# A subtraction emitted one product later in the MLP units of a hybrid decoder trunk

## The chip, the cores and the metric

The kernel runs on one core of a Trainium2 chip. The metric is the device time of one execution in microseconds (us). The engines are named as the profile names them: PE is TensorE (matmuls), PEld its weight loads, DVE is VectorE, ACT is ScalarE, POOL is GpSimd, and SP is SyncE, whose queue issues the DMAs.

## The reference

The reference is a decoder trunk of two layers over 528 tokens (16 meta tokens and 512 of the sequence) of width 1024. Layer 0 mixes with retention and gated DeltaNet heads, layer 1 with a Mamba-2 mixer. Behind each mixer stands a layer norm and an MLP with a squared ReLU, which is all that matters here:

```python
def sq_relu_mlp(h, w1, w2):
    return jnp.square(jax.nn.relu(h @ w1)) @ w2
...
h = layer_norm(DN_ALPHA * h + sq_relu_mlp(h, mlp_w1[i], mlp_w2[i]), ln2_w[i], ln2_b[i])
```

`w1` is 1024 x 4096 and `w2` 4096 x 1024.

## The kernel before, in words

**Split numbers.** All large products run on numbers that are split into a high part, rounded to the matmul's format, and a low part, the rest. A product of two such numbers takes three matmuls: high by high, high by low, low by high. Weights are split as they arrive: ScalarE rounds (line 152) and VectorE subtracts (line 153, function `split`). Activations are split where they are made.

**The MLP.** Features of the hidden layer are made in eight groups of four blocks of 128. Group 0 and half of group 1 are made by plain products (`phase`, lines 609 to 618). All other halves of groups, 13 per MLP and so 26 in the kernel, are made by a `Unit`: two blocks of 128 features by two halves of the tokens (264 columns each in layer 0, 256 in layer 1), by a fast scheme of seven products instead of eight. Each of the seven is 12 matmuls (line 514: four blocks of the contraction by three). They write to three PSUM banks in turn: `ba` (products 1, 3, 5, 7), `bc_` (2, 6) and `bb` (4). ScalarE copies `ba`, `bc_`, `ba` after products 1 to 3 (lines 518, 521, 524) into `x1`, `x2`, `x3`. VectorE adds product 4, 5 and 6 to these (lines 527, 531, 535). In order: product 4 onto `bb`, sum of line 527, output; product 5 onto `ba`, sum of line 531, output; product 6 onto `bc_`, sum of line 535, output; product 7 onto `ba`, output. `ba` keeps accumulating, so the seventh product adds to what the sum of line 531 reads.

**The output (`evac_u`).** For each of the four outputs ScalarE takes the ReLU (line 451), GpSimd squares it in full precision (line 453, into a tile `q`), ScalarE squares it into the high part (line 459), and VectorE subtracts the high part from `q` to give the low part (line 460). That last subtraction is what the change moves. `q` is a tile of the tag "m", which has 24 buffers; the high and low parts are of tag "s" with 40.

**The second product.** A stage `Four` multiplies four blocks of `w2` with a finished group and adds the result to the residual on VectorE (line 383; for a first contribution, line 385). Stages alternate: a `Unit` of group c, a `Four` of group c-1, and so on. In layer 0 a `Four` has matmuls of 272 and 256 columns, in layer 1 of 512.

**What sets the order.** The code emits instructions in an order written out by hand. After each product, and after each half of a block in a `Four`, it calls `adv`, which takes the next stage's preparation (weight fetches, additions of lines 487 to 491, splits) one step on and gives waiting tasks a turn (`tick`). A planner then orders each engine's instructions when the program is compiled: it runs through the program by durations of its own and gives an engine the earliest emitted of the instructions that are ready in its run, so the order on an engine can differ from the order of emission. On the chip each engine keeps the planner's order.

Of the kernel before, what the change touches and what calls it, by code (L numbers as in the profile page):

```python
# [12 lines left out]
F32 = mybir.dt.float32  # L13
# [3 lines left out]
ADD, SUB, MUL, MIN, MAX, POW = ALU.add, ALU.subtract, ALU.mult, ALU.min, ALU.max, ALU.pow  # L17
# [40 lines left out]
def trunk(ctx: ExitStack, tc: tile.TileContext, a, out):  # L58
    nc = tc.nc
    V, G, S, T, SY = nc.vector, nc.gpsimd, nc.scalar, nc.tensor, nc.sync  # L60
# [11 lines left out]
    def tl(tag, cols, dt=F32, part=P):  # L72
        return sb.tile([part, cols], dt, tag=tag, bufs=NBUF[tag], name=nm(tag))
# [4 lines left out]
    def pm(cols, part=P):  # L78
        return ps.tile([part, cols], F32, tag="mm", bufs=3, name=nm("pmm"))
# [30 lines left out]
    def tick():  # L110
        for gen in list(tasks):
            if gen in tasks:
                advance(gen)
# [117 lines left out]
    def parts(pair, spans):  # L231

        return [tuple(x[:, o:o + n] for x in pair) for o, n in spans]
# [189 lines left out]
    def mlp(l, hx, h, ns, ready, evac0, pairs, final=None):  # L423
# [4 lines left out]
        nh = (ns[0] + ns[1]) // 2  # L428
# [12 lines left out]
        def group():  # L441
            u = [[None] * GF for _ in hx]
            us = [None] * GF

            def evac_u(f, hf, o, n=None):
                if n is None:
                    n, off = ns[hf], hf * ns[0]
                else:
                    off = hf * n
                t = tl("m", n)  # L450
                S.activation(t, o, AF.Relu)  # L451
                q = tl("m", n)
                G.tensor_tensor(q, t, t, op=MUL)  # L453
                if us[f] is None:
                    us[f] = pair = tl("s", L, F32R), tl("s", L, F32R)
                    for dst, x in zip(u, parts(pair, ((0, ns[0]), (ns[0], ns[1]), (0, 512)))):
                        dst[f] = x
                hi, lo = [x[:, off:off + n] for x in us[f]]
                S.activation(hi, t, AF.Square)
                V.tensor_tensor(lo, q, hi.bitcast(F32), op=SUB)  # L460
            return u, evac_u

        def second_src(c, m):
# [2 lines left out]
        class Unit:  # L466
# [7 lines left out]
            def prepare(self):  # L474
# [26 lines left out]
                self.ops["s4"] = sp(s4)  # L501

            def run(self, adv):
                ba, bb, bc_ = pm(nh), px(nh), px(nh)
                row = tl("row", 1024)
# [11 lines left out]
                prod(ba, "a11", 0, True, False)  # L517
                S.copy(x1, ba)
                adv()
                prod(bc_, "s1", 4, True, False)  # L520
                S.copy(x2, bc_)
                adv()
                prod(ba, "s2", 5, False, False)
                S.copy(x3, ba)
# [62 lines left out]

        groups = [group() for _ in range(NG)]

        def unit(c, i):  # L590
            return Unit(c, i, lambda f, hf, o: groups[c][1](f, hf, o, nh))

        def four(c, i):
            return Four(c, groups[c][0], 4 * i)

        stages = [unit(1, 1), four(0, 0), four(0, 1)]
        for c in range(2, NG):
            stages += [unit(c, 0), four(c - 1, 0), unit(c, 1), four(c - 1, 1)]
# [23 lines left out]
        for i, st in enumerate(stages):  # L622
            if i + 2 < len(gens):
                next(gens[i + 2])

            def adv():
                next(gens[i + 1], None)
                tick()
            st.run(adv)
            for _ in gens[i + 1]:  # L630
                pass
        for _ in gens[-1]:
            pass
        if final is not None:
            final(groups[-1][0][2], last[0].blks, h)
            return
# [537 lines left out]
    r, ev = accumulate(r0)  # L1174
    hn, hx, ready1 = norm_after(r, ns0, PP_LN + 16, PP_LN + 24)
    mlp(0, h, r0, ns0, ready, ev, hp)
    h = hn

# [200 lines left out]
    for g in range(4):  # L1379
        f = []  # L1380
# [20 lines left out]
    for m in range(3):  # L1401
        blks = wload(srcs[m][0]) + wload(srcs[m][1][:, 0:512], 512)
        o = pm(512)
# [13 lines left out]
    def final(u, blks, r):  # L1417
# [41 lines left out]
        with tc.manual_schedule(engines=ORDERED):  # L1459
# [12 lines left out]
            store(3, 512, 704, t1[:, 0:192])  # L1472

    mlp(1, h, r0, ns1, ready, ev, hp, final)
    drain()

# [100 lines left out]
```

## Time and profile before

| | us |
|---|---|
| runs | 1718.58 (median), 1712.72, 1718.89 |
| profiled execution | 1710.59 |
| its span | 1708.8 |
| granted TensorE clock, mean | 0.994 |
| TensorE busy | 1662.7 (97%) |
| VectorE busy | 1154.1 (68%) |
| ScalarE busy | 739.0 (43%) |
| GpSimd busy | 316.9 (19%) |

The first MLP runs from about 530 to 890 us of the span, its units from 575 us on; the second from about 1360 us, its units from 1380 to 1665 us. A pair of `Unit` and `Four` repeats every 22.7 us in layer 0 (L553's fetches start at 656.49 and 679.19) and every 21.8 us in layer 1.

How to read the rows. A timeline row has the start in us from the span's start, the duration in us, the engine, the line of the kernel, the operation, the tiles written and read, the shapes and the number of instructions merged into the row; in brackets the idle time of that engine before it and what ended it. A row of the waits reads: engine, line, who was waited for, total us, number of times, the longest. A matmul's row lasts longer than the distance to the next one, since matmuls are pipelined.

### The profile page before, as it was taken

To read this page: it belongs to the slowest core of one execution; us is meant where nothing else is said; L and a number is where in the kernel's file an instruction comes from. 1 tells how busy PE (TensorE), PEld (TensorE's weight loads), DVE (VectorE), ACT (ScalarE), POOL (GpSimd) and SP (SyncE) were. 2 spreads that over 40 slices of the span, in tenths; PEclk is the share of its full clock that TensorE was granted. 3 is DMA by queue.
4 is the path that set the end of the run, shared out by engine and by line. 5 is a ranking of instruction groups with operands and counts; after the bars stand their busy time and mean duration, and the time that the engine had idled before them with its cause. 6 is when DMAs were issued, how large, how long until landed. Compare 5 with 4: busy or idle time off the path is not lost.

```text
span 1708.8 us, 29912 instructions
## 1 busy us (share of the span) xinstructions
PE 1662.7 (97%) x11884; PEld 1529.0 (89%) x11884; DVE 1154.1 (68%) x2300; ACT 739.0 (43%) x1509; POOL 316.9 (19%) x360
## 2 busy tenths in 40 slices
PE   9899999999999999999999999999999999999998
PEld 7898998899999999999998988888778888888886
DVE  5896667666437857766657776858553876666665
ACT  4432245554214534444434665656432544444441
POOL 1211210010003301111102034242410321111112
PEclk9999999999999999999999999999999999999999
DMA  6233212112222322222221443333222222222231
GB/s 219 83 95 93 70 38 69 50 51 79 95 75 69 106 93 96 81 97 99 88 71 63 139 117 110 108 111 112 68 86 96 79 99 93 98 94 96 92 116 49
DMA packets 88484, 155.60 MB, mean 91 GB/s; under 512 B 11864, under 2 KB 43224, under 8 KB 88344
## 3 DMA queue, kind: packets, MB, share of 16 engines
q1 hardware_dynamic: 88200, 153.53, 28.1%
q8 instruction: 93, 1.52, 0.4%
q14 instruction: 47, 0.39, 0.1%
q10 hardware_dynamic: 144, 0.16, 0.0%
HBM read 148.92 MB, written 4.75 MB: 90 GB/s over the span
## 4 chain that ended last, share of the span: by engine, by line
PE 81%; DVE 8%; ACT 3%; POOL 3%; issue 2%; DMA 2%; SPq 0%; POOLq 0%; DVEq 0%; ACTq 0%
PE pmm L178 19%; PE pmm L177 19%; PE pmm L176 19%; PE pmm L514 7%; PE pmx L514 4%; POOL m L453 2%; ACT w L152 1%; DVE w L153 1%; PE pmx L1439 1%; DVE s L650 1%; DMA w<-in_w 1%; PE pmx L1289 1%; ACT m L451 1%; DVE s L460 1%; PE pmx L1293 1%
## 5 line engine op out<-in xcount | busy, mean ns | idle before, releaser
L176 PE MATMUL pmm<-hh,w 128*128 128x256 f32 (+5 forms) x1480 | 455.2, 308 | 5.6 <-ACT s L643 2.0
L178 PE MATMUL pmm<-hh,w 128*128 128x256 f32 (+3 forms) x1480 | 443.4, 300 | 0.2 <-DVE w L153 0.2
L177 PE MATMUL pmm<-hl,w 128*128 128x256 f32 (+3 forms) x1480 | 442.0, 299 | 1.2 <-DVE hl L344 0.9
L153 DVE TENSOR_TENSOR w<-w,w 128x1024 fp32r<-128x1024 f32 (+2 forms) x253 | 312.3, 1236 | 147.7 <-PE pmm L177 79.8
L152 ACT CAST w<-w 128x1024 fp32r<-128x1024 f32 (+2 forms) x253 | 260.9, 1032 | 347.5 <-PE pmm L177 88.9
L176 PE MATMUL pmm<-s,w 128*128 128x256 f32 (+2 forms) x1136 | 361.2, 318 | 0.0
L178 PE MATMUL pmm<-s,w 128*128 128x256 f32 (+2 forms) x1136 | 360.8, 318 | 0.0
L177 PE MATMUL pmm<-s,w 128*128 128x256 f32 (+2 forms) x1136 | 360.3, 317 | 0.0
L176 PEld LDWEIGHTS pmm<-hh,w 128*128 128x128 f32 (+2 forms) x1480 | 279.0, 189 | 19.5 <-issue 4.2
L177 PEld LDWEIGHTS pmm<-hl,w 128*128 128x128 f32 (+1 forms) x1480 | 278.8, 188 | 12.5 <-issue 2.1
L178 PEld LDWEIGHTS pmm<-hh,w 128*128 128x128 f32 (+1 forms) x1480 | 279.0, 189 | 8.8 <-DVE w L153 0.7
L177 PEld LDWEIGHTS pmm<-s,w 128*128 128x128 f32 x1136 | 213.7, 188 | 14.3 <-DVE s L1368 0.3
L176 PEld LDWEIGHTS pmm<-s,w 128*128 128x128 f32 x1136 | 213.9, 188 | 14.0
L178 PEld LDWEIGHTS pmm<-s,w 128*128 128x128 f32 x1136 | 213.7, 188 | 14.1
L453 POOL TENSOR_TENSOR m<-m 128x256 f32<-128x256 f32 (+2 forms) x128 | 117.1, 917 | 534.3 <-ACT m L451 530.8
L147 POOL TENSOR_TENSOR n<-n,neg 128x1 f32<-128x1 f32 (+2 forms) x58 | 40.3, 699 | 439.3 <-DVE n L146 418.7
L650 DVE SCALAR_TENSOR_TENSOR s<-s,pp,s 128x528 f32<-128x528 f32 x120 | 102.2, 851 | 27.1 <-ACT s L648 24.9
L383 DVE TENSOR_TENSOR m<-m,pmm 128x272 f32<-128x272 f32 (+1 forms) x208 | 81.7, 415 | 19.1 <-PE pmm L178 19.0
L460 DVE TENSOR_TENSOR s<-m,s 128x256 fp32r<-128x256 f32 (+2 forms) x128 | 64.9, 508 | 43.9 <-POOL m L453 41.5
L514 PE MATMUL pmm<-s,s 128*128 128x264 f32 (+1 forms) x624 | 83.8, 283 | 0.1
L514 PEld LDWEIGHTS pmm<-s,s 128*128 128x128 f32 x624 | 78.5, 188 | 0.5 <-DVE s L153 0.3
L527 DVE TENSOR_TENSOR row<-row,pmx 128x264 f32<-128x264 f32 (+1 forms) x26 | 11.0, 424 | 97.2 <-PE pmx L514 97.2
(313 smaller groups left out, 2464.8 us busy)
## 6 DMA issues: line engine op xcount, KB each, us to landing
w<-in_w SPq DMA_DIRECT2D x88, 512.0 KB, 3.2
w<-in_mw SPq DMA_DIRECT2D x146, 256.0 KB, 3.1
w<-in_mw SPq DMA_DIRECT2D x38, 512.0 KB, 3.3
w<-in_wo SPq DMA_DIRECT2D x29, 512.0 KB, 3.3
row<-rd SPq DMA_DIRECT2D x16, 512.0 KB, 5.6
sp<-in_mw SPq DMA_DIRECT2D x26, 256.0 KB, 2.7
s<-rd SPq DMA_DIRECT2D x32, 128.0 KB, 5.8
w<-in_w2n SPq DMA_DIRECT2D x4, 512.0 KB, 3.2
```

The source lines that it names most:

```text
L147: G.tensor_tensor(dst, t, neg5[0:part, 0:n], op=POW)
L152: S.copy(dst_hi, src)
L153: V.tensor_tensor(dst_lo, src, dst_hi.bitcast(F32), op=SUB)
L176: T.matmul(o, w[0], x[0], start=first, stop=False)
L177: T.matmul(o, w[0], x[1], start=False, stop=False)
L178: T.matmul(o, w[1], x[0], start=False, stop=last)
L383: V.tensor_tensor(t, t, o, op=ADD)
L451: S.activation(t, o, AF.Relu)
L453: G.tensor_tensor(q, t, t, op=MUL)
L460: V.tensor_tensor(lo, q, hi.bitcast(F32), op=SUB)
L514: T.matmul(o, w[x][:, c], B[b][k][y], start=first and k == i == 0, stop=last and k == 3 and i == 2, skip_group_check=True)
L650: V.scalar_tensor_tensor(acc, cin[:, k:k + L], w[k], acc, op0=MUL, op1=ADD)
```

## The change

The low parts of the units' four outputs are no longer subtracted inside `evac_u`. The operands are put on a list, and `adv` emits what was put there one product earlier. So the low part of an output is emitted after the sum and the output of the following product. That of product 7 is emitted in the first `adv` of the next stage. The two plain phases, which do not pass a list, stay as they are.

```diff
-            def evac_u(f, hf, o, n=None):
+            def evac_u(f, hf, o, n=None, late=None):
...
                 S.activation(hi, t, AF.Square)
-                V.tensor_tensor(lo, q, hi.bitcast(F32), op=SUB)
+                if late is None:
+                    V.tensor_tensor(lo, q, hi.bitcast(F32), op=SUB)
+                else:
+                    late[-1].append((lo, q, hi.bitcast(F32)))
...
+        late = [[], []]
+
+        def lower():
+            for lo, q, hi in late.pop(0):
+                V.tensor_tensor(lo, q, hi, op=SUB)
+            late.append([])
+
         def unit(c, i):
-            return Unit(c, i, lambda f, hf, o: groups[c][1](f, hf, o, nh))
+            return Unit(c, i, lambda f, hf, o: groups[c][1](f, hf, o, nh, late))
...
             def adv():
+                lower()
                 next(gens[i + 1], None)
                 tick()
             st.run(adv)
...
         for _ in gens[-1]:
             pass
+        lower()
+        lower()
         if final is not None:
```

## The prediction

> **What bounds the kernel now.** I read the page's busy shares first, then TensorE's waits, then the chain of waits and the engines' timelines in one repeat of the multilayer perceptron (MLP).
>
> ```profile
> PE 1662.7 (97%) x11884; PEld 1529.0 (89%) x11884; DVE 1154.1 (68%) x2300; ACT 739.0 (43%) x1509; POOL 316.9 (19%) x360
> ...
> PE pmm L514 <- DVE row L531: 14.5, 26, 2.1
> PE pmx L1053 <- DVE m L1098: 2.8, 1, 2.8
> ...
> PE pmm L514 <- DVE row L531: 6.3, 12, 0.6
> ...
> PE pmm L514 <- DVE row L531: 5.6, 12, 0.5
> ...
> DVE s L460 <- POOL m L453: 41.5, 62, 0.9
> ```
>
> TensorE is busy 97% of the span, so time can only come from its gaps. The largest wait of TensorE by far is on line 531, VectorE's sum behind a unit's fifth product: 26 times, once in each of the 26 units; the next is a fifth of it. Two answers for stretches of the two MLPs, 605 to 890 and 1375 to 1660 us, show that 12 of the waits in each are alike (0.53 and 0.47 us in the mean); the first unit of layer 0 and the last of layer 1 stand outside of them. These rows count a wait from the end of a matmul's record, which lasts some 0.28 us while the next matmul can start 0.12 us after it, so that the time lost is larger than 14.5 us; it is worked out below from starts. Line 460, the subtraction that the change moves, waits for GpSimd's square on line 453. How the two are connected is seen in the repeat from 656 to 679 us:
>
> ```profile
> 662.13 1.64 PE L514 MATMUL pmm<-s,s 128*128 128x264 f32 x12
> ...
> 664.95 0.28 PE L514 MATMUL pmx<-hh,s 128*128 128x264 f32 x1
> 665.06 0.29 PE L176 MATMUL pmm<-s,w 128*128 128x272 f32 x1
> 665.87 0.51 PE L514 MATMUL pmm<-s,w 128*128 128x264 f32 x2 [0.51 <-DVE row L531]
> ...
> 664.95 0.19 PEld L176 LDWEIGHTS pmm<-s,w 128*128 128x128 f32 x1
> 665.86 0.30 PEld L514 LDWEIGHTS pmm<-s,w 128*128 128x128 f32 x2 [0.73 <-DVE row L531]
> ...
> 662.40 0.43 DVE L527 TENSOR_TENSOR row<-row,pmx 128x264 f32<-128x264 f32 x1 [4.41 <-PE pmx L514]
> 663.29 1.23 DVE L153 TENSOR_TENSOR w<-w,w 128x1024 fp32r<-128x1024 f32 x1 [0.46 <-ACT w L152]
> 665.04 0.43 DVE L460 TENSOR_TENSOR s<-m,s 128x264 fp32r<-128x264 f32 x1 [0.52 <-POOL m L453]
> 665.39 0.42 DVE L531 TENSOR_TENSOR row<-row,pmm 128x264 f32<-128x264 f32 x1
> 665.73 0.42 DVE L535 TENSOR_TENSOR row<-row,pmx 128x264 f32<-128x264 f32 x1
> 667.07 0.43 DVE L460 TENSOR_TENSOR s<-m,s 128x264 fp32r<-128x264 f32 x1 [0.92 <-POOL m L453]
> ...
> 663.66 1.34 POOL L453 TENSOR_TENSOR m<-m 128x264 f32<-128x264 f32 x1 [17.30 <-ACT m L451]
> 668.43 0.63 POOL L453 TENSOR_TENSOR m<-m 128x264 f32<-128x264 f32 x1 [0.45 <-ACT m L451]
> ```
>
> The fifth product of the unit ends at 662.13+1.64 = 663.77; from then on line 531 has its input. VectorE is in the weight split of line 153 until 663.29+1.23 = 664.52. Then comes line 460 for the fourth product, which waits until GpSimd's square is ready (663.66+1.34 = 665.00), and line 531 stands behind it: it starts at 665.39, 0.87 us after the split ended. The seventh product adds onto the bank that line 531 reads, so its weight load starts only at 665.86. TensorE has put in one matmul of the next stage (line 176, at 665.06) and then starts nothing until 665.87.
>
> **The change part by part.** It removes and adds no instruction. In each unit the four line 460 subtractions are emitted one product later: 26x4 = 104 moves, the same operands, the same 0.43 us. Line 460 of product 4 goes behind line 531, that of product 5 behind line 535, that of product 6 behind product 7, and that of product 7 behind the first product and sum (line 383) of the following stage. The last is also emitted behind the weight fetches with which that stage begins on SyncE's queue; SyncE waits for nothing of it, and no DMA is moved. On GpSimd nothing is passed that waits for line 460.
>
> Step 1, does VectorE's order follow? A planner orders VectorE: it takes a ready instruction ahead of one that it thinks not ready, as the rows show, where line 535 runs ahead of product 5's line 460, which the code emits earlier. Line 460 of product 4 must therefore have been ready in the plan when it was taken, and the code's order decided only if line 531 was ready too. On the chip line 531 has been ready for 664.52-663.77 = 0.75 us when the split ends. The plan has just one line 176 matmul between the sixth and seventh product, so its line 531 ends about when the sixth ends, 1.45 us (12 matmuls) after the fifth ended; line 460 starts in it some 0.35+0.42 us earlier, about 0.7 us after line 531's input. Both were ready, so the later emission swaps them.
>
> Step 2, what line 531 then costs. It starts as the split ends, at 664.44 (consecutive VectorE rows overlap by 0.08), and ends at 664.86. That GpSimd's square is running there must be allowed for. The nearest row is line 1326, of the same engine with one PSUM operand and 256 columns, of which the first instance below lies inside one GpSimd instruction and the third has none beside it:
>
> ```profile
> 1025.18 0.41 DVE L1326 SCALAR_TENSOR_TENSOR s<-m,pmm 128x256 f32<-128x256 f32 x1
> ...
> 1041.79 0.41 DVE L1326 SCALAR_TENSOR_TENSOR s<-m,pmm 128x256 f32<-128x256 f32 x1
> ...
> 1024.13 2.03 POOL L1302 TENSOR_TENSOR s<-s,s 128x512 f32<-128x512 f32 x1
> ```
>
> Both take 0.41 us, so I take 0.42 for line 531. The other end is that it waits for the square to finish: it then ends at 665.00+0.42 = 665.42. No reason makes it shorter than 0.41. [...]
>
> Step 3, does TensorE still wait? A weight load followed the end of line 531 by 0.05 us (665.81 to 665.86). From 664.86 that gives 664.91, and the free weight load after the sixth product is at 664.95: no wait in layer 0. So each of the 12 regular units there gives 665.87-665.06 = 0.81 less the usual 0.12 between matmuls, 0.69 us. In layer 1 the stage's matmuls have 512 columns:
>
> ```profile
> 1443.88 0.40 PE L176 MATMUL pmm<-s,w 128*128 128x512 f32 x1
> 1444.74 0.62 PE L514 MATMUL pmm<-s,w 128*128 128x256 f32 x3 [0.46 <-DVE row L531]
> ...
> 1442.20 1.23 DVE L153 TENSOR_TENSOR w<-w,w 128x1024 fp32r<-128x1024 f32 x1 [0.47 <-ACT w L152]
> ...
> 1446.44 0.23 PE pmm L177
> ...
> 583.83 0.28 PE L177 MATMUL pmm<-s,w 128*128 128x272 f32 x1
> 586.21 0.63 PE L514 MATMUL pmm<-s,w 128*128 128x264 f32 x3 [2.09 <-DVE row L531]
> ...
> 583.65 1.22 DVE L153 TENSOR_TENSOR w<-w,w 128x1024 fp32r<-128x1024 f32 x1
> ...
> 585.73 0.42 DVE L531 TENSOR_TENSOR row<-row,pmm 128x264 f32<-128x264 f32 x1
> ...
> 1662.43 0.40 PE L178 MATMUL pmm<-s,w 128*128 128x512 f32 x1
> 1663.27 0.75 PE L514 MATMUL pmm<-s,w 128*128 128x256 f32 x4 [0.43 <-DVE row L531]
> ```
>
> Its 12 regular units give 1444.74-1443.88 = 0.86 less the usual 0.23 of such a matmul, 0.63 us each. Line 531 would end at 1442.20+1.23-0.08+0.42 = 1443.77 and allow a weight load at 1443.82; a free one stands 0.11 ahead of 1443.88, at 1443.77, so at worst 0.05 us is left per unit. The first unit of layer 0 waits longer, since its split also comes late: line 531 moves from 585.73 to 583.65+1.22-0.08 = 584.79, 0.94 us, and the rest of its gap stays. The last unit of layer 1 gives 1663.27-1662.43 = 0.84 less 0.23, 0.61 us.
>
> Sum: 12x0.69 + 12x0.63 + 0.94 + 0.61 = 8.3+7.6+0.9+0.6 = 17.4 us, less up to 13x0.05 = 0.65 for layer 1: 17.0 us.
>
> Step 4, what the moved instruction costs where it lands. Product 4's line 460 still starts at about 665.02, when the square is ready, now behind line 531; line 535 follows at 665.37 instead of 665.73, and ScalarE's activations behind lines 531 and 535 come 0.95 and 0.36 us earlier. The lower parts are first read by a stage that runs after a further unit, over 10 us later. I cost this at nothing; what hides it is that distance and the idle 0.52 and 0.92 us ahead of line 460, and if that cover were gone, each moved instruction would cost VectorE its 0.43 us. Buffers: an output holds two of 24 "m" tiles, of which 16 are the residual; the 8 left serve four outputs, all that a unit has. Late next is TensorE itself, with matmuls at their usual distance through the unit.
>
> The profiled execution took 1710.59 us for its span of 1708.8, so it would take 1693.6. It is the lowest of the four times shown: the three runs have 1712.72, 1718.58 (the median) and 1718.89. From the median the sum gives 1701.6, from the mean of the four (1715.2) 1698.2. I forecast 1700.
>
> **The rivals.** (a) The order stays as it was, because in the plan line 460 is taken before line 531 has its input, by shorter times for the square than the chip's. For it: the chip's square takes twice as long beside the split as at 668.43, and a plan may not know that. Against it: the 0.7 us of step 1. Then the time is as before, 1712 to 1719. (b) Line 531 has to wait for the square after all (the other end of step 2): the weight load comes at 665.47 instead of 665.86, a gain of 0.39 us in 25 units and at most 0.94 in the first, 10.7 at most and some 9 us with a later plan: 1708 to 1709. Against it speaks line 1326. (c) Slower: with the new emission the plan fills VectorE's idle places with the preparation of the next unit, and the sums of the following stage (line 383) come later. The rows:
>
> ```profile
> 668.71 0.29 PE L178 MATMUL pmm<-s,w 128*128 128x272 f32 x1
> ...
> 667.42 1.12 DVE L491 TENSOR_TENSOR s<-w,sp 128x512 f32<-128x512 f32 x1
> ...
> 669.27 0.68 DVE L153 TENSOR_TENSOR s<-sp,s 128x512 fp32r<-128x512 f32 x1
> 669.87 0.42 DVE L383 TENSOR_TENSOR m<-m,pmm 128x272 f32<-128x272 f32 x1
> ```
>
> The first product of that stage ends about 669.0, its sum starts at 669.87, 0.9 us later; with three banks TensorE can run two products (2x1.45 = 2.9 us) ahead of a sum. Were line 491 and three splits of 512 columns (1.12+3x0.68 = 3.2 us) all put ahead of the first sum, it would be 4.1 us late and TensorE would wait 1.2 us per unit, 26x1.2 = 31 us, against the 17 gained: 1718.6+14 = 1733. It decides from 2.0 us of delay on, and makes the kernel slower than before from 2.0+17/26 = 2.7 us on. Against it: line 491 and one of the splits are ahead of that sum already, and VectorE's work in the stage begins 0.95 us earlier.
>
> **How the numbers follow.** My forecast 0.73, (a) 0.13, (b) 0.07, (c) 0.07. A difference of 0.5% is 8.6 us, about what a measurement of this kernel can tell from no change. Faster by more than that: the forecast and half of (b), 0.77; within it: (a) and the other half, 0.16; slower: (c), 0.07. The range takes in the forecast from its low end (1710.6-17.4 = 1693, with a margin of 1) and (b) up to 1709 with a margin of 2: 1692 to 1711, which leaves out (a) and (c).
>
> **What would show it.** On VectorE's timeline line 531 follows the split of line 153 directly and line 460 comes behind it, still waiting for GpSimd; TensorE's wait on line 531 falls from 14.5 us to under 2.5, almost all of it in the first unit; a repeat of unit and stage shortens from 22.7 us to 22.0 in layer 0; line 453 leaves the chain in favour of TensorE; line 383 is no later behind its product than before. The prediction is wrong if line 460 is still ahead of line 531, if line 531 takes more than 0.45 us, or if a new wait of TensorE on lines 176 to 178 or 514 has over 5 us.

## The result, and the profile after

| | before | after |
|---|---|---|
| runs, median (us) | 1715.65 (1709.34 to 1718.89, 4 runs) | 1691.51 (1689.14 to 1691.81, 4 runs) |
| profiled execution (us) | 1710.59 | 1691.81 |
| its span (us) | 1708.8 | 1690.0 |

The ratio after to before is 0.9861, with a 95% interval of 0.9827 to 0.9895: 24 us by these medians, 18.8 us by the two profiled spans. Both are more than the 17.0 us of the prediction's sum, and the time lies 0.5 us below the range. In the changed file the lines stand three (in the unit) lower: L517 is the old L514, L530, L534 and L538 are the sums of products 4, 5 and 6 (old L527, L531, L535), and L597 is the moved subtraction (old L460).

The page after: busy time of each engine, and the chain of work that ended last (before it had PE 81% and POOL 3%).

```profile
PE 1655.9 (98%) x11884; PEld 1528.5 (90%) x11884; DVE 1159.4 (69%) x2300; ACT 740.2 (44%) x1509; POOL 313.9 (19%) x360
...
PE 87%; DVE 7%; ACT 2%; DMA 2%; issue 1%; POOL 1%; SPq 0%; POOLq 0%; DVEq 0%; ACTq 0%
```

TensorE's waits after, the five largest:

```profile
PE pmm L176 <- ACT w L152: 3.5, 1, 3.5
PE pmx L1302 <- DVE s L1263: 2.8, 3, 1.3
PE pmx L801 <- DVE n L793: 2.6, 1, 2.6
PE pmx L1066 <- DVE m L1111: 2.6, 1, 2.6
PE pmm L517 <- DVE row L534: 2.0, 1, 2.0
```

The wait on product 5's sum is there once instead of 26 times, in the first unit, and in the MLPs no wait of its size has come in its place. The repeat that the prediction read, whose fifth product starts 0.9 us earlier in the span now (661.23 against 662.13), on the timelines of TensorE, VectorE and GpSimd:

```profile
661.23 1.64 PE L517 MATMUL pmm<-s,s 128*128 128x264 f32 x12
...
664.04 0.28 PE L517 MATMUL pmx<-hh,s 128*128 128x264 f32 x1
664.16 1.63 PE L517 MATMUL pmm<-s,w 128*128 128x264 f32 x12
665.63 0.29 PE L176 MATMUL pmm<-s,w 128*128 128x272 f32 x1
...
662.39 1.23 DVE L153 TENSOR_TENSOR w<-w,w 128x1024 fp32r<-128x1024 f32 x1 [0.46 <-ACT w L152]
663.53 0.42 DVE L534 TENSOR_TENSOR row<-row,pmm 128x264 f32<-128x264 f32 x1
664.36 0.43 DVE L538 TENSOR_TENSOR row<-row,pmx 128x264 f32<-128x264 f32 x1 [0.41 <-PE pmx L517]
664.71 1.04 DVE L597 TENSOR_TENSOR s<-m,s 128x264 fp32r<-128x264 f32 x2
...
668.09 0.42 DVE L383 TENSOR_TENSOR m<-m,pmm 128x272 f32<-128x272 f32 x1
...
662.87 1.23 POOL L453 TENSOR_TENSOR m<-m 128x264 f32<-128x264 f32 x1 [17.52 <-ACT m L451]
```

Line 534 starts 0.09 us before the split's row ends (662.39+1.23 = 663.62) and takes 0.42 us inside GpSimd's square (662.87 to 664.10). It is done at 663.95, before the sixth product's last matmul starts at 664.04, and the seventh product follows 0.12 us after that. Line 538 runs ahead of the moved subtractions, which stand in one row with those of product 5.

Beside it the same product before, and the pair in layer 1 (before, then after):

```profile
665.06 0.29 PE L176 MATMUL pmm<-s,w 128*128 128x272 f32 x1
665.87 1.75 PE L514 MATMUL pmm<-s,w 128*128 128x264 f32 x12 [0.51 <-DVE row L531]
...
1444.74 1.69 PE L514 MATMUL pmm<-s,w 128*128 128x256 f32 x12 [0.46 <-DVE row L531]
```

```profile
1432.59 0.28 PE L517 MATMUL pmx<-hh,s 128*128 128x256 f32 x1
1432.71 1.64 PE L517 MATMUL pmm<-s,w 128*128 128x256 f32 x12
...
1432.20 0.41 DVE L534 TENSOR_TENSOR row<-row,pmm 128x256 f32<-128x256 f32 x1
...
1432.66 0.42 PEld L517 LDWEIGHTS pmm<-s,w 128*128 128x128 f32 x3
```

The twelve matmuls of product 7 last 1.75 us behind a wait and 1.63 us without one in layer 0, 1.69 and 1.64 in layer 1. That is a loss that the prediction did not see. In layer 1 a small wait is left: the weight load of product 7 starts at 1432.66, 0.05 us after the sum's end (1432.20+0.41 = 1432.61), and the second matmul of product 7 comes 0.17 us after the first, where 0.12 is usual. Over all regular units, by TensorE's starts:

| mean, us | layer 0 before | after | layer 1 before | after |
|---|---|---|---|---|
| last start of product 6 to first of product 7 | 0.934 | 0.119 | 0.980 | 0.117 |
| first to third start of product 7 | 0.350 | 0.244 | 0.343 | 0.282 |
| one repeat of `Unit` and `Four` | 22.715 | 21.931 | 21.807 | 21.107 |

Before, the first row of this table holds one matmul of the next stage (0.12 us in layer 0, 0.23 in layer 1), which stands elsewhere after; so it is not all loss, and the last row is the gain.

### The profile page after: what moved, and what is told of

The parts are those of the page before. It is cut to its first block, busy times and chain, and to the rows that moved or that the text cites. A ratio compares the mean times of both kernels' runs of the same rounds, so it can differ in the third digit from the quotient of the medians.

```text
span 1690.0 us, 29900 instructions
## 1 busy us (share of the span) xinstructions
PE 1655.9 (98%) x11884; PEld 1528.5 (90%) x11884; DVE 1159.4 (69%) x2300; ACT 740.2 (44%) x1509; POOL 313.9 (19%) x360
## 4 chain that ended last, share of the span: by engine, by line
PE 87%; DVE 7%; ACT 2%; DMA 2%; issue 1%; POOL 1%; SPq 0%; POOLq 0%; DVEq 0%; ACTq 0%
PE pmm L176 20%; PE pmm L178 20%; PE pmm L177 20%; PE pmm L517 9%; PE pmx L517 6%; PE pmx L1452 1%; DVE w L153 1%; DMA w<-in_w 1%; DVE s L663 1%; PE pmx L1306 1%; PE pmx L1302 1%; PE pmx L274 1%; DVE m L343 1%; POOL n L147 1%; PE pmx L334 1%
## 5 line engine op out<-in xcount | busy, mean ns | idle before, releaser
L383 DVE TENSOR_TENSOR m<-m,pmm 128x272 f32<-128x272 f32 (+1 forms) x208 | 82.7, 416 | 19.1 <-PE pmm L178 18.8
L517 PE MATMUL pmm<-s,s 128*128 128x264 f32 (+1 forms) x624 | 83.6, 283 | 0.5 <-ACT row L521 0.4
L517 PEld LDWEIGHTS pmm<-s,s 128*128 128x128 f32 x624 | 78.5, 188 | 0.9 <-ACT row L521 0.6
L530 DVE TENSOR_TENSOR row<-row,pmx 128x264 f32<-128x264 f32 (+1 forms) x26 | 11.0, 425 | 97.4 <-PE pmx L517 97.4
L597 DVE TENSOR_TENSOR s<-m,s 128x264 fp32r<-128x264 f32 (+1 forms) x104 | 61.9, 613 | 3.2 <-ACT m L451 1.3
```

The source lines that it names most:

```text
L383: V.tensor_tensor(t, t, o, op=ADD)
L517: T.matmul(o, w[x][:, c], B[b][k][y], start=first and k == i == 0, stop=last and k == 3 and i == 2, skip_group_check=True)
L597: V.tensor_tensor(lo, q, hi, op=SUB)
```

## The experiments

"Early" is the kernel before, "late" the changed one. Runs of the early order that stood beside these had medians of 1713.4 to 1716.8 us.

**The two kernels again.** They stand here for their spread.

> The kernel before, unchanged, as its own control. Its runs so far spread from 1709.3 to 1718.9 us, while those of the changed kernel lie within 2.7 us. Theory: a ratio of 1.000 and a profile with the same gaps of TensorE as the one shown (some 0.8 us lost at each of 26 units); if a profile of 1716 us or more comes, its units have the same gaps and the extra 8 us stand in another place. Rival: the extra time of the longer runs stands in the units' gaps too, so that part of the run-to-run spread is of the thing that the change takes away.

1712.59 us (1708.25 to 1716.94, 12 runs), ratio 0.999 (0.9976 to 1.0005); span of the profile 1706.5.

> The changed kernel once more, as control beside the others: 1691 us, ratio 0.986.

1691.0 us (1689.8 to 1692.28, 4 runs), ratio 0.9861 (0.9837 to 0.9884); span 1689.5. The early order scatters over 9 us, the late one over 2.5, in fewer runs.

**Which of the four moves matters.** In the late order, the condition of the new branch:

```diff
-                if late is None:
+                if late is None or not (f < 2 and hf == 0):   # only product 4 late
```

> Only the low part of product 4 is emitted late; those of products 5, 6 and 7 stay where they were. Theory (the stall is line 531 standing behind that one subtraction): the whole gain, 1691 us, the same 0.12 us between the sixth and seventh product. Rival (the gain, larger than the sum by 1.4 us in the span, comes in part from the other three moves): 1695 to 1700 us.

1691.72 us (1689.55 to 1692.19, 4 runs), ratio 0.9863 (0.9842 to 0.9883), span 1690.0. The opposite:

```diff
-                if late is None:
+                if late is None or f < 2 and hf == 0:          # all but product 4
```

> The low parts of products 5, 6 and 7 are emitted late, that of product 4 stays. Theory: no gain, 1710 to 1719 us, and a wait of TensorE of about 14.5 us on the sum behind the fifth product. Rival (the other moves give part): 5 us or more below the kernel before.

1714.12 us (1709.67 to 1718.43, 10 runs), ratio 0.9997 (0.9983 to 1.0011). VectorE's timeline has the old order:

```profile
665.21 1.23 DVE L153 TENSOR_TENSOR w<-w,w 128x1024 fp32r<-128x1024 f32 x1 [0.46 <-ACT w L152]
666.95 0.43 DVE L461 TENSOR_TENSOR s<-m,s 128x264 fp32r<-128x264 f32 x1 [0.52 <-POOL m L453]
667.30 0.42 DVE L534 TENSOR_TENSOR row<-row,pmm 128x264 f32<-128x264 f32 x1
```

Product 4's subtraction (here L461) waits for the square with the sum L534 behind it. The whole gain is that of one subtraction in four.

**The same place on VectorE's queue by another way.** The early order of emission, with the units' subtraction on GpSimd:

```diff
+                eng = V if n is None else G
...
-                V.tensor_tensor(lo, q, hi.bitcast(F32), op=SUB)
+                eng.tensor_tensor(lo, q, hi.bitcast(F32), op=SUB)
```

> The order of emission is that of the kernel before, but the units' 104 low parts are subtracted on GpSimd, so that VectorE has no subtraction ahead of the sum behind the fifth product. Theory (only the place of that subtraction on VectorE's queue counts): the same 1691 us as the change, with GpSimd busier by about 104 x 0.63 = 66 us. Rival 1 (VectorE's load in the units counts too): below 1688 us. Rival 2 (GpSimd becomes late with the squares): a new wait, 1695 us or more.

1692.97 us (1687.71 to 1693.18, 4 runs), ratio 0.9863 (0.9839 to 0.9886), span 1691.3.

```profile
660.53 1.22 DVE L153 TENSOR_TENSOR w<-w,w 128x1024 fp32r<-128x1024 f32 x1 [0.46 <-ACT w L152]
661.68 0.42 DVE L532 TENSOR_TENSOR row<-row,pmm 128x264 f32<-128x264 f32 x1
```

The sum (L532) stands behind the split again and the gain is the same. What counts is that the subtraction is not ahead of the sum; the time that VectorE saves besides brings nothing.

**The square doubled.** In units GpSimd squares twice, the second time over the first result:

```diff
                 G.tensor_tensor(q, t, t, op=MUL)
+                if twice:
+                    G.tensor_tensor(q, t, t, op=MUL)
```

> The kernel before, with GpSimd's square of each unit output computed twice into the same tile. On VectorE the subtraction still stands ahead of the sum in 25 of the 26 units. Theory (TensorE waits for GpSimd through that subtraction): the sum comes later by a second square of 0.6 us, 25 x 0.6 = 15 to 16 us more, 1727 to 1731 us, and the loss right after each wait (0.35 us instead of 0.24 between the first and third matmul of the seventh product) stays 0.11 us, as it does not depend on the wait's length. Rival (the wait is for the weight split, not for GpSimd): no more than 1720 us. The runs between 1709 and 1719 us of the kernel before are spread by stretches at half TensorE clock of 3.4 or 6.8 us; if longer waits bring these on, the spread grows or such stretches appear among the units.

1739.48 us (1736.67 to 1742.64, 4 runs) against 1716.8 of the early order beside it, ratio 1.0142 (1.0119 to 1.0165): 22.7 us more, where less was expected.

> The changed kernel with the same doubled squares. Theory (the sum no longer depends on GpSimd): no change of the time, 1691 us within 2. Rival (the moved subtractions only have a little slack and hold VectorE up further on): 1695 us or more, with waits of TensorE on line 383's sums or on weight splits.

1701.8 us (1700.81 to 1703.42, 4 runs), ratio 0.992 (0.9897 to 0.9942) to the early order, so some 10 us above the late order: a miss. In the early order:

```profile
668.81 0.29 PE L176 MATMUL pmm<-s,w 128*128 128x272 f32 x1
670.31 1.75 PE L517 MATMUL pmm<-s,w 128*128 128x264 f32 x12 [1.21 <-DVE row L534]
...
669.48 0.43 DVE L463 TENSOR_TENSOR s<-m,s 128x264 fp32r<-128x264 f32 x1 [1.22 <-POOL m L456]
669.83 0.42 DVE L534 TENSOR_TENSOR row<-row,pmm 128x264 f32<-128x264 f32 x1
...
PEld pmm L176 <- DVE m L383: 5.4, 22, 0.3
```

The mean gap ahead of product 7 grows by 0.70 us in both layers (0.934 to 1.636, 0.980 to 1.680): the chain from square to subtraction to sum to TensorE is confirmed. The matmuls of product 7 last 1.75 us as before, behind a wait of 1.21 us instead of 0.51, so what was lost behind the wait did not grow with it. But layer 0's repeat grew by 1.39 us (24.10), twice as much; the last row, a wait of the weight loads from 620 to 870 us, names the rest: the sums of line 383. For the regular units that is 24x0.70+12x0.69 = 25.1 us, against 1734.9-1708.8 = 26.1 between the spans; besides, the first unit takes 3.6 us more, the last 0.9 less (in it the sum now stands ahead of the subtraction), and the stretches outside of the units 1.7 less. In the late order that wait is there too, and it is all of the 10 us:

```profile
663.93 0.42 DVE L537 TENSOR_TENSOR row<-row,pmm 128x264 f32<-128x264 f32 x1
...
665.23 0.84 DVE L600 TENSOR_TENSOR s<-m,s 128x264 fp32r<-128x264 f32 x1
666.59 0.84 DVE L600 TENSOR_TENSOR s<-m,s 128x264 fp32r<-128x264 f32 x1 [0.52 <-POOL m L456]
667.36 1.11 DVE L497 TENSOR_TENSOR s<-w,sp 128x512 f32<-128x512 f32 x1
668.39 0.85 DVE L600 TENSOR_TENSOR s<-m,s 128x264 fp32r<-128x264 f32 x1
669.17 1.11 DVE L153 TENSOR_TENSOR s<-sp,s 128x512 fp32r<-128x512 f32 x1
670.20 0.42 DVE L383 TENSOR_TENSOR m<-m,pmm 128x272 f32<-128x272 f32 x1
...
670.33 0.28 PE L178 MATMUL pmm<-s,w 128*128 128x272 f32 x1
670.68 0.39 PE L176 MATMUL pmm<-s,w 128*128 128x256 f32 x1
...
PEld pmm L176 <- DVE m L383: 7.2, 23, 0.3
```

Two things delay VectorE. Product 5's subtraction waits 0.52 us for GpSimd, and two kinds of its instructions take longer beside the squares, of which there are now twice as many: the subtraction (L600 here) 0.84 or 0.85 us instead of 0.43, a split of 512 columns 1.11 instead of 0.68. The first sum of the `Four` starts 670.20-663.93 = 6.27 us behind the sum of product 5 (L537 here), 1.71 us later than in the profile after (668.09-663.53 = 4.56), and TensorE, which would start at 670.45, pauses until 670.68. Layer 0's repeat is 22.73 instead of 21.93, layer 1's 21.09 as before. This is the mechanism of rival (c), sums that come late, in small.

**The first unit.** Its 0.94 us were part of the sum. VectorE, before and then after:

```profile
582.10 0.69 DVE L487 TENSOR_TENSOR w<-sp,w 128x512 f32<-128x512 f32 x1 [2.74 <-DMA w<-in_mw]
582.71 0.42 DVE L527 TENSOR_TENSOR row<-row,pmx 128x264 f32<-128x264 f32 x1
```

```profile
583.44 0.69 DVE L490 TENSOR_TENSOR w<-sp,w 128x512 f32<-128x512 f32 x1 [3.38 <-DMA w<-in_mw]
584.05 0.42 DVE L530 TENSOR_TENSOR row<-row,pmx 128x264 f32<-128x264 f32 x1
...
584.99 1.22 DVE L153 TENSOR_TENSOR w<-w,w 128x1024 fp32r<-128x1024 f32 x1
586.12 0.42 DVE L534 TENSOR_TENSOR row<-row,pmm 128x264 f32<-128x264 f32 x1
```

An addition for the next unit (old L487, now L490) waits for a fetched weight ahead of the first unit's sums. That fetch landed later in the second profile, so TensorE's pause only went from 2.62 to 2.32 us. Two kernels order this addition, and two of its neighbours, behind product 5's sum:

```diff
+                with tc.issue_after(sums[0]) if sums else ExitStack():
                     V.tensor_tensor(s1, a21, a22, op=ADD)
                     V.tensor_tensor(s3, a11, a21, op=SUB)
...
+                with tc.issue_after(sums[0]) if sums else ExitStack():
                     V.tensor_tensor(s2, s1, a11, op=SUB)
...
                 V.tensor_tensor(x2, x2, ba, op=ADD)
+                sums.append(nc.cur_bb.bb.instructions[-1])
```

> The changed kernel, in which VectorE's additions of the next unit's weights (lines 490, 491, 493) are ordered behind the first unit's sum after its fifth product, since the first of them waits for a DMA and stands ahead of that unit's sums. Theory: the first unit's wait of TensorE (2.0, 0.4 and 2.6 us in three profiles of the late order) goes, about 2 us in the mean, 1689 us; the spread of the runs is no larger. Rival (the DMA is then waited for a little later): no change, 1691 us.

1691.0 us (1689.75 to 1694.07, 4 runs), ratio 0.9861 (0.984 to 0.9882), span 1688.6. The wait is gone:

```profile
581.11 1.23 DVE L153 TENSOR_TENSOR w<-w,w 128x1024 fp32r<-128x1024 f32 x1 [0.46 <-ACT w L152]
582.25 0.42 DVE L538 TENSOR_TENSOR row<-row,pmm 128x264 f32<-128x264 f32 x1
```

The sum of product 5 (here L538) follows its split at once, and the second unit starts 33.6 us after the first instead of 35.9. The runs do not show these 2.3 us.

> The kernel before with the order of the seventh experiment in the first unit only: VectorE's additions for the next unit's weights behind the sum after the fifth product. What is open is why the runs of the early order spread over 9 us and lie up to 3 us further above those of the late order than their profiles do. Theory (part of the spread is the DMA that the first unit's sums wait for; TensorE waited 2.1, 1.1 and 3.5 us there in three profiles of the early order): the wait falls to under 0.8 us, the runs come down by 1 to 2 us and spread over 6 us or less. Rival (the spread is from elsewhere): the same 1709 to 1719 us.

1710.97 us (1707.73 to 1714.52, 12 runs) against 1714.9 beside it, ratio 0.9977 (0.9963 to 0.9991), span 1708.5. In the early order the same edit is worth 4 us of the median, more than expected, and the runs scatter over 7 us instead of 10.

**What scatters.** The kernel before, three more times.

> The kernel before once more, for another profile of its spread. Theory: the regular units repeat every 22.71 and 21.81 us as in the three profiles of the early order; what differs between profiles is the first unit's wait and the number of stretches of 3.4 us at half clock. Rival: the repeats themselves differ.

> As the run before this one: the same repeats, another first unit's wait and another number of stretches at half clock.

> As the run before this one: the same repeats, another first unit's wait and another number of stretches at half clock.

1717.91, 1714.62 and 1715.63 us, spans 1716.1, 1712.8 and 1713.8. The repeats of the two MLPs are the same in all early profiles (22.712 to 22.722 and 21.802 to 21.814 us). Two things differ: the wait in the first unit, and stretches in which TensorE is granted half its clock. The first is the longest wait in TensorE's row on line 531, here in the repeat of the early order above (span 1706.5) and in the second of these three runs (span 1712.8):

```profile
PE pmm L514 <- DVE row L531: 13.5, 26, 1.1
PE pmm L514 <- DVE row L531: 16.1, 26, 3.7
```

For the second, here is the layer norm behind the first MLP, 900 to 930 us (time, busy time of PE, PEld, DVE, ACT and POOL with their counts, granted clock, DMA share, GB/s), in the profile of before, in that of the second of these three runs, and in that after:

```profile
900.00:930.00 30.00, 28.23 (x219) 25.28 (x218) 23.54 (x60) 15.35 (x27) 9.90 (x15) 1.00 0.11 36
```

```profile
900.00:930.00 30.00, 28.35 (x198) 25.05 (x198) 20.83 (x55) 10.83 (x17) 7.36 (x11) 0.89 0.16 52
```

```profile
900.00:930.00 30.00, 28.27 (x222) 25.40 (x222) 23.88 (x56) 17.17 (x33) 9.46 (x20) 1.00 0.18 59
```

In the second one the clock is 0.89: half of it for 6.8 us from 915.2 on, and some 20 matmuls fewer in the 30 us. Between 50 and 1600 us all such stretches in all profiles last 3.4 or 6.8 us; matmuls of 256 columns stand 0.21 us apart in them instead of 0.12. Within an execution they lie whole multiples of 3.41 us apart (154.64, 550.59 and 1356.13 in the profile of before, 116 and 236 times 3.413 us from one to the next). Each of these three lasts 3.41 us, at a granted clock of 0.50; a stretch of that length is called a window below.

In these profiles TensorE pauses 1.3 to 1.4 us in that layer norm. Where the pause began 0.2 to 0.9 us after a multiple, the stretch followed in five of six profiles, and in none elsewhere. The last four kernels move it, by k matmuls of 272 columns that the next product overwrites, ahead of the last `Four` of layer 0:

```diff
                             o = pm(ns[hf])
+                            if final is None and self is stages[-1] and j == 0 and hf == 0:
+                                for _ in range(k):
+                                    T.matmul(o, self.blks[j][0][:, 0:P], self.u[hf][0][0], start=True, stop=True, ...)
                             product(o, [self.blks[j]], self.u[hf])
```

> The late order with ten more matmuls of 272 columns (0.125 us each, overwritten by the product that follows) ahead of the last second-product stage of the first MLP, so that the layer norm behind it comes 1.25 us later. In the profiles so far TensorE pauses 1.3 to 1.4 us in that layer norm; where the pause begins 0.1 to 0.9 us after a multiple of 3.413 us counted from an earlier half-clock stretch of the same execution, a half-clock stretch of 6.8 us followed in five of six profiles; where it begins 1.1 us or more after (seven profiles), in none. Theory, phase: the late order's pause, which begins 2.4 to 3.0 us after a multiple, moves to 0.2 to 0.8, the stretch appears and the time is 1691.4+1.25+2.75 = 1695.4. Rival, the stretch belongs to the early order of VectorE and not to the phase: no stretch, 1692.6.

1697.04 us (1696.32 to 1700.68, 6 runs), ratio 0.9893 (0.9875 to 0.991), span 1695.1.

> The late order with 27 such matmuls, 27x0.125 = 3.4 us, a whole period: the phase stays. Phase: no stretch in the layer norm, 1691.4+3.4 = 1694.8. Rival (any delay of the layer norm brings the stretch): 1697.5.

1695.22 us (1694.56 to 1700.98, 6 runs), ratio 0.9888 (0.9867 to 0.9909), span 1693.1.

> The early order (the kernel before) with 15 such matmuls, 1.9 us. Phase: the pause, which begins 0.1 to 1.6 us after a multiple, moves to 2.0 to 3.5, the stretch goes from most executions, and the time is 1713.4+1.9-(some two thirds of 2.75) = 1713.5. Rival, the stretch belongs to the early order: it stays, 1715.3.

1718.13 us (1716.86 to 1723.85, 12 runs) against 1714.24 beside it, ratio 1.0022 (1.0007 to 1.0036), span 1715.1.

> The early order with 27 such matmuls, a whole period. Phase: the stretch stays as frequent as before, 1713.4+3.4 = 1716.8. Rival, that a later layer norm escapes it: 1714.9.

1717.9 us (1713.48 to 1721.25, 12 runs), ratio 1.0016 (1.0002 to 1.003), span 1711.7.

None of the four profiles has the stretch in the layer norm. In all four the pause begins 2.0 to 2.6 us after a multiple, also where 10 matmuls were to bring it to 0.2 to 0.8: the profiled execution's windows lay 2.0 us otherwise against its start than those of the profile after, so the trial of the late order did not take place. The rival, that the stretch belongs to the early order, is not decided either: these two early orders, the profile of before and the repeat of span 1706.5 are without it, but no profile of a late order has it. A whole period costs about its matmuls, 3.4 us, in both orders (1691.4 to 1695.2, where the 1691.4 was not run beside it, and 1714.2 to 1717.9). Parts of a period cost more than theirs: 1.25 us of matmuls cost 5.6, 1.9 us cost 3.9. Those two profiles have stretches elsewhere: at 586.5 and 586.8 us, ahead of the added matmuls, and behind them at 968.8 and 979.3. There TensorE's longest wait on a copy of ScalarE (line 659 in the late order, 646 in the early) was 4.1 and 3.5 us (1.4 in the profiles of before and after); so what these two kernels pay includes longer waits, and is not the half clock alone. The latter place, from 960 to 985 us, in the late order with 10 matmuls and in the profile after:

```profile
960.00:985.00 25.00, 20.86 (x153) 19.58 (x152) 13.72 (x18) 20.37 (x45) 0.30 (x1) 0.93 0.65 175
```

```profile
960.00:985.00 25.00, 23.62 (x185) 22.38 (x184) 18.68 (x22) 20.12 (x45) 3.30 (x2) 1.00 0.52 160
```

Counting the half-clock windows of 3.4 us between 50 and 1600 us of each profile, and taking the added matmuls off the spans:

| windows | early: spans (us) | late: spans (us) |
|---|---|---|
| 2 | | 1689.5 |
| 3 | 1706.5, 1708.8, 1708.3 | 1690.0, 1690.0, 1689.7 |
| 4 | 1713.8, 1713.2 | 1693.9 |
| 5 | 1712.8, 1712.8 | |
| 6 | 1716.1 | |

The early column is the profile of before, the repeats, all but product 4, and 15 and 27 matmuls; the late one is the profile after, its repeat, only product 4, and 10 and 27 matmuls. At three windows the orders differ by 1707.9-1689.9 = 18.0 us, at four by 1713.5-1693.9 = 19.6. The early profiles have 4.1 windows in the mean, the late ones 3.0, and from three to six the early span grows by 8.2 us. But that growth is not the windows' alone. The early order without the first unit's wait has five windows too, and a span of 1708.5. And the same stretch of matmuls, compared with the lightest early profile (1706.5), takes this much longer or shorter (us):

| profile (span) | 545 to 560 | first unit | layer norm | 1340 to 1380 | all else |
|---|---|---|---|---|---|
| before (1708.8) | 0.0 | +1.0 | 0.0 | +1.1 | +0.2 |
| first of the three (1716.1) | -1.6 | +5.0 | +2.8 | +1.2 | +2.3 |
| second (1712.8) | -1.6 | +4.1 | +2.7 | 0.0 | +1.1 |
| third (1713.8) | -1.6 | +4.0 | +2.8 | 0.0 | +2.1 |

The lightest has a window at 550 us that the last three lack: it costs 1.6 us. One at 1356 and 1364 us costs 1.1 to 1.2, the two of the layer norm 2.7 to 2.8. The largest part is the first unit: its wait is 1.1 us in the lightest and 3.6 to 3.7 in the last three, with a half-clock window at the wait's end (two in the first of the three). All five early profiles of four windows or more have a wait of 3.4 us or more there, the three lightest 1.1 to 2.1.

## Why the prediction was right or wrong

**Steps 1 and 2, the order and the sum: right.** In all 26 units the sum of product 5 comes ahead of the moved subtraction, and it takes 0.41 to 0.42 us inside the square. Rivals (a) and (b) are out. (Of the rows of line 1326 that the prediction shows, the one without GpSimd beside it is that at 1041.79.)

**Step 3, no wait: right but for 0.05 us; its terms, 0.69 and 0.63 us per unit: too small, and this put the time out of the range.** They counted the gap and not the slower start behind it. The repeats show 22.715-21.931 = 0.78 and 21.807-21.107 = 0.70 us. Most of the missing 0.09 and 0.07 is that the first to third start of product 7 takes 0.244 instead of 0.350 us, and 0.282 instead of 0.343. This loss was readable before: 0.35 us for two distances that are 0.12 each elsewhere. The up to 0.05 us left per unit in layer 1 did come: it is in the 0.17 us between the first two matmuls of product 7, which is why layer 1's 0.282 is above layer 0's 0.244. Regular units give 12x0.78+12x0.70 = 17.8 us instead of 15.9 less 0.65. (The prediction's 17.4 less 0.65 is 16.7; its 17.0 stands between the two.) The low end of the range was the lightest time shown less this sum and a margin of 1, 1710.6-17.4-1 = 1692.2. With the 18.7 us that all units gave it is 1690.9, and the 1691.5 measured lies above it.

**The first unit's 0.94 us: not gained.** The prediction took the rest of its gap to stay, and it did not: the weight of the next unit's addition landed 1.34 us later against the span's start (583.44 against 582.10), while the unit itself began 0.7 us later, and the wait ate the gain. TensorE's wait there is 0.4 to 3.0 us in the late profiles. That it is absent in the kernel of the first unit without a faster run says that it was no safe term either way. **The last unit's 0.61** came as 0.9 (1.41+0.34 to 0.59+0.25). So 17.8+0.9 = 18.7 against 18.8 measured between the spans. That these agree to 0.1 us is partly luck: outside of the units the two profiles differ both ways; the profile after takes 0.9 us more in its first 20 us, and 1.2 us less at 1356 us, where only the profile of before has a half-clock window.

**The base: why the forecast of 1700 was 8.5 us too high.** Of these, 1.7 are the sum's (17.0 instead of 18.7). The rest is the base of 1717 from which the sum was taken, as though the early runs' scatter would remain in the late order. In the changed kernel it did not: its eight runs lie within 3.1 us, though the late orders with added matmuls scatter over 4 and 6. A sum with its size put right, taken from the profile of before alone, meets the runs, 1710.6-18.7 = 1691.9; but that profile was the second lightest of five of its kernel, so that this too is partly luck. Over all runs of the two kernels (89 and 8) the medians are 1714.2 and 1691.3, which is 22.9 us apart, 4 more than the units gave.

Where these 4 us lie is shown in part only. The mean granted clock of 85 early runs is 0.9931, that of the eight late ones 0.9946, which is about one and a half half-clock windows of 3.41 us less in 1700 us; by the 1.1 to 1.6 us that a single window cost above, some 2 us. The other measure is the first unit: taking the wait out of it brought the early order 4 us and the late one nothing that its runs show, and with that edit in both the orders are 1711.0-1691.0 = 20.0 us apart (19.9 by their ratios to the early order beside each, 0.9977 and 0.9861). The two overlap, since in the early profiles a long wait there comes with a window. Why the late order pays less for the first unit, whose wait is 0.4 to 3.0 us in its profiles against 1.1 to 3.7, and why it has no stretch in the layer norm, stays open. The position of a pause against the period fits the layer norm in all profiles but one (only product 4 late, 0.8 us after a multiple, no stretch), and the kernel that was to prove it in the late order landed elsewhere.

**Step 4, the landing place: right in cost, wrong in order and in its cover.** The prediction put the moved subtraction at 665.02 with line 535 behind it. Line 538 runs ahead of it, in every unit, at no cost. But the cover named, over 10 us until the low parts are read and VectorE's idle 0.5 and 0.9 us, is not the one that counts. VectorE's queue also leads to the sums of line 383, and with the doubled square, which delays the first of them by 1.7 us, TensorE already loses 0.80 us per unit of layer 0. Rival (c) did not happen, and it stood nearer than the 2.0 us of delay that the prediction gave it from the banks alone.

**What would show it.** The wait under 2.5 us and in the first unit alone (2.0), the repeat at 22.0 (21.93), line 453 gone from the chain's list, and the first sum of line 383 0.8 us behind its product instead of 0.9: as said.

## What to carry to other kernels

When an instruction that waits for a slow engine stands in order ahead of one that TensorE waits for, price the move by the start-to-start distance of the matmuls around the gap, from the last one ahead of it to the third behind it, so that the slow restart (here 0.35 us for two distances instead of 0.24) is counted too. Before a sum is subtracted from a time, see by two or three profiles of the same kernel what scatters between its runs, place by place and not by the count of half-clock stretches alone, and whether the profile in hand is a light or a heavy one. And leave room in the range for an error in a term that is taken many times: 0.08 us in each of 24 units was 1.9 us here. VectorE's idle place was cover here only up to the next instruction on its queue that TensorE needed: with the sums of line 383 1.71 us later, layer 0 lost 0.80 us per unit.

## What the runs showed of the hardware

- Behind a wait of 0.5 to 1.2 us, the first two distances of the next matmuls took 0.35 us together where they take 0.24 without one (layer 0); behind 0.7 us more of waiting the twelve matmuls took the same 1.75 us.
- The granted clock falls to one half (0.50 from 154.64 to 158.05 us in the profile of before) for 3.4 or 6.8 us in the middle of a kernel that is 97% busy. In such a stretch matmuls of 256 columns stand 0.21 us apart instead of 0.12; a single window of 3.41 us cost 1.1 to 1.6 us where it stood between busy matmuls, two in a row 2.7 to 2.8. One followed a wait of TensorE of only 0.9 us (at 550 us). The windows of an execution lie on one grid of 3.41 us; against the span's start it lay 0.32 us later in the profile after than in that of before (154.96 and 154.64).
- Beside GpSimd's squares the moved subtraction took up to 0.85 us instead of 0.43 and a split of 512 columns 1.11 instead of 0.68 (both with the doubled square in the late order, the former also in the profile after). In the repeats shown the split of 1024 columns took 1.23 us beside the square (1.22 at the median in the profile after), and it was the square that took 1.34 us before and 1.23 after, against 0.63 at 668.43 in the profile of before. The sum of product 5 took 0.41 to 0.42 us inside the square in all 26 units after.
